# A hybrid trunk on one core: the first MLP's second product as seven block products, with x turned back afterwards

## The chip, the cores and the metric

The kernel runs on one core of one Trainium2 chip. The metric is the device time of one launch in microseconds (us); the kernel before was timed three times, 1201.20, 1201.91 and 1201.94, median 1201.91 us.

## The reference

A decoder trunk of two layers on 512 tokens with 1024 channels, all in fp32. Every mixer and every MLP adds to the residual stream x:

```
x = x + even_mixer(rmsnorm(x))      # an S5 scan and dilated attention, one output projection
x = x + relu(rmsnorm(x) @ w1[0])**2 @ w2[0]
x = x + odd_mixer(rmsnorm(x))       # mLSTM: matrix memory, exponential gates, chunks
x = x + relu(rmsnorm(x) @ w1[1])**2 @ w2[1]
```

w1 is 1024 x 4096 and w2 4096 x 1024 in each layer. The change is in the second line and in the beginning of the third.

## The kernel before, in words

**Data.** x lies in SBUF as eight tiles of 128 channels x 512 tokens (`self.x[k]`, tags x0 to x7). A step `prep(k, gi)` (line 189) makes of a tile the gained hi and lo halves `hg[k]` (ACT line 117, then DVE line 108) and adds its squares to `ss`; the norm's factor itself is applied later, after a product. An fp32 product is the sum of three products in a rounded type: weight hi x activation hi, hi x lo, lo x hi. One such matmul is 128 x 128 weights against 512 columns.

**Weights** come as units of 512 KB (`wr`, 128 x 1024 fp32), in the order of `unit_list`. `w_pump` (line 151) loads up to four units ahead through SP's queue, and splits up to three ahead: ACT makes `wh` (line 120), DVE makes `wl` (line 96). The sets of buffers are taken in turn by the unit's index modulo 3.

**The order** of each engine's instructions is set by a scheduler that simulates the program's timeline when it is built; the code's order is its start. Engines then work through their own queues in that order.

**The first MLP** (`mlp`, line 261) works in two halves of the 4096 hidden channels. 16 units give relu and square of 16 hidden tiles each half, split into `sh` and `sl` at once; 8 pairs of units then give the second product for eight tiles of x, 48 matmuls each, weights stationary. Each result is scaled by `r2` (the squared norm, spread over 128 rows by `norm_finish_sq` and four matmuls) and added to x; in the second half `prep(m, 2)` follows at once, so that the odd layer's input is made tile by tile.

**The second MLP** (`mlp_rows`, line 377) makes all 32 hidden tiles first and keeps them unsplit (`s0` to `s31`). Its second product is turned around: tokens are stationary, weights move, and the result is tokens x channels. It treats hidden tokens and w2 as 2 x 2 blocks and needs seven block products of 96 matmuls in place of eight (`PRODS`, in the order 1, 4, 6, 7, 5, 2, 3). Four of the seven take sums of weight blocks: `t_sums` (line 289) loads four blocks (`tq`), makes four sums on DVE, stores them to DRAM (`T`) and reads them back later as units. `prod_unit` (line 321) splits each activation block into `sp` hi (ACT, line 120) and lo (DVE, line 96) with a ring of five tiles, and updates the raw blocks on DVE for the products to come. `x_rows` (line 303) turns x to token rows with PE transposes (line 307) and `prod_out` (line 345) adds the scaled products to those rows, which are written out as they become whole.

**The odd layer** (`odd`, line 1084) follows a string, `ODD_SEQ` (line 28): `z` is the gates' product, `v0` to `v7` the V units (four units fill four accumulators `acc`, then ACT copies them to V), `N` the norm's finish, `g` the gates, `c` the turn of the gate columns to `col` (lines 1066 and 1068), `q`, `k`, `s`, `n`, `o`, `h` the steps of a head. `q` loads two rows that the gates wrote to DRAM (`na`, `it`); `s` makes the scores' factor `dx` and `qi`. PSUM has four `acc` buffers, two `psa` and two `psb`. `self.skip` (line 83) takes a gap in a pool and clears it on POOL.

Of the kernel before, what the change touches and what calls it, by code (L numbers as in the profile page):

```python
# [9 lines left out]
F32 = mybir.dt.float32  # L10
# [17 lines left out]
ODD_SEQ = ("z0 v0 N0 g0 v1 v2 v3 q0 c0 k0 q1 s0 k1 n0 q2 s1 k2 n1 o0 h0 q3 s2 k3 n2 o1 h1 q4 s3 k4 n3 "  # L28
# [33 lines left out]
class Trunk:  # L62
# [198 lines left out]
    def mlp(self, nxt):  # L261
        with self.tc.tile_pool(name="mp", bufs=1) as mp:
            for half in range(2):
                s = []
                for m in range(16):
                    z = self.proj(self.hg)
                    if half == 0 and m == 1:
                        r2 = self.norm_finish_sq()
                    rr = self.tmp("rr")
                    self.act(rr, z, AF.Relu)  # L270
                    sh = self.t(mp, (P, T), f"sh{m}", F32R)
                    sl = self.t(mp, (P, T), f"sl{m}", F32R)
                    self.act(sh, rr, AF.Square)
                    sf = self.tmp("sf")
                    self.mul(sf, rr, z)
                    self.sub(sl, sf, sh.bitcast(F32))
                    s.append((sh, sl))
                for m in range(KT):
                    o = self.proj(s, first=True, last=False, ks=range(0, 8))
                    self.proj(s, acc=o, first=False, last=True, ks=range(8, 16))  # L280
                    e = self.tmp("ev", bufs=3)
                    self.mul(e, o, r2)
                    self.add(self.x[m], self.x[m], e)
                    if half == 1:
                        self.prep(m, nxt)

    TS_AT = (2, 5, 8, 11, 14, 17, 20, 23)

    def t_sums(self, mp, u):
        q = [self.t(mp, (P, 1024), f"tq{n}", bufs=1) for n in range(4)]  # L290
        for n in range(4):
            self.dma(q[n], self.a["w2s"][n, u])
# [5 lines left out]
        for n, r in ((1, b11), (3, b12), (2, b22), (4, b21)):  # L298
            d = self.t(self.dp, (P, 1024), f"T{n}_{u}", bufs=1)
            self.dma(d, r)  # L300
            self.tq[n, u] = d

    def x_rows(self, i):
# [4 lines left out]
        if n == 0:  # L308
            r = self.tmp(("ss", "r", "sf", "sf")[t], bufs=(1, 1, 2, 2)[t])
        else:  # L310
            r = self.xt(t)
        self.copy_act(r, p)
        self.xr[t, n] = r

# [30 lines left out]
    def prod_out(self, i, accs):  # L345
        def up(t, n, y, c):
            x = self.xr[t, n]
            self.stt(x, y, c[:, t:t + 1], x, ALU.mult, ALU.add)
            if i in self.DONE[t // 2, n]:
                self.dma(self.out[2 * t + n], x)  # L350
# [26 lines left out]
    def mlp_rows(self):  # L377
        self.tq, self.xr, self.pe, self.pv = {}, {}, {}, {}
        with self.tc.tile_pool(name="mp", bufs=1) as mp:
            self.sq = []  # L380
            p1 = None
            for m in range(32):
# [12 lines left out]
                if 2 <= m < 10:  # L395
                    self.x_rows(m - 2)
                if m in self.TS_AT:
                    self.t_sums(mp, self.TS_AT.index(m))
# [3 lines left out]
            self.prod_out(1, p1)  # L402
            for i in self.PRODS[1:]:
# [3 lines left out]
                self.prod_out(i, accs)  # L407

    def rows_units(self):
        a = self.a  # L410
        un = []
        for m in range(32):
            un.append(a["w1"][1, m])
            if m > 16 and m % 2:
                un.append(a["w2s"][0, (m - 17) // 2])
        src = {4: 4, 6: 2, 7: 3, 5: 1, 2: None, 3: None}
        for i in self.PRODS[1:]:
            q = src[i]
            for u in range(8):
                if i == 2:  # L420
                    un.append(a["w2s"][2, u])
                elif i == 3:
                    un.append(a["w2s"][3, u])
                else:
                    un.append(lambda q=q, u=u: self.tq[q, u])
# [515 lines left out]
    def even(self):  # L941
# [4 lines left out]
        with ExitStack() as es:  # L946
# [37 lines left out]
            def s5_done():  # L984
                s5s.close()
                self.ap = es.enter_context(self.tc.tile_pool(name="at", bufs=1))
                self.skip(self.ap, 128)
# [96 lines left out]
    def odd(self):  # L1084
# [4 lines left out]
        self.skip(mp, 96)  # L1089
# [27 lines left out]
        def z_part(_):  # L1117
            z = self.proj(self.hg)
# [111 lines left out]
    def run(self):  # L1230
# [30 lines left out]
        self.hg = [None] * KT  # L1261

# [4 lines left out]
        self.mlp(2)  # L1267
# [5 lines left out]
        self.mlp_rows()  # L1273

    def unit_list(self):
# [8 lines left out]
        mlp = lambda l: [a["w1"][l, h * 16 + m] if ph == 0 else a["w2"][h, m] for h in range(2) for ph in range(2) for m in range(16)]  # L1284
        units += mlp(0)
# [3 lines left out]
        units += self.rows_units()  # L1289
# [115 lines left out]
```

## Time and profile before

| what | value |
|---|---|
| median of 3 runs | 1201.91 us |
| profiled execution | 1202.68 us |
| its span | 1200.9 us |
| TensorE (PE) busy | 1177.3 us, 98% |
| VectorE (DVE) busy | 736.8 us, 61% |
| ScalarE (ACT) busy | 574.4 us, 48% |
| moved by DMA | 170.41 MB, mean 142 GB/s |
| first MLP, first to last matmul | 350.08 us |
| odd layer's mixer up to its output projection | 214.64 us |
| second MLP, first to last matmul | 331.97 us |

The profile is of one execution; the span runs from its first to its last instruction and is 1.8 us shorter than the time of the launch. The page lists busy time by engine, the chain that ended last and the costliest groups; windows give the same counters for a stretch of the span. PE's matmuls overlap, so the record of one (0.39 us) is longer than the step from one to the next. The granted clock is TensorE's, as a share of its full 2.4 GHz.

### The profile page before, as it was taken

What the parts mean: (1) busy time and instruction counts of PE and PEld (TensorE: products, weight loads), DVE (VectorE), ACT (ScalarE), POOL (GpSimd) and SP (SyncE); (2) the same over time, 40 slices, a digit from 0 to 9 for tenths busy, and PEclk for the clock granted to TensorE, in tenths of its full rate; (3) what the DMA queues carried; (4) which work ended last, traced back from release to release, by engine and by line L of the source; (5) the groups of instructions that cost most, each with busy time, mean ns of one, the idle gap of its engine ahead of it and who ended that gap; (6) DMA issues with size and microseconds to landing.
All of it is one profiled execution on the core that took longest, in us unless ns stands there. A gap on an engine that the chain in (4) does not pass through costs nothing.

```text
span 1200.9 us, 15231 instructions
## 1 busy us (share of the span) xinstructions
PE 1177.3 (98%) x5580; PEld 968.8 (81%) x5580; DVE 736.8 (61%) x1307; ACT 574.4 (48%) x1009; POOL 65.4 (5%) x122
## 2 busy tenths in 40 slices
PE   6989999999999999999999999999999999999998
PEld 5868776788888888888888888887888888888887
DVE  8799864554443344435449773874665564477796
ACT  5467777443432133423336554454344344466664
POOL 0522220000000000000010000000000000000000
PEclk9989999999999999999999999999999999999999
DMA  6434522333323333232334333321499995346664
GB/s 233 123 89 124 144 75 62 114 106 94 100 91 102 101 93 104 90 104 89 103 95 152 105 106 106 93 75 45 164 350 365 349 344 176 118 148 195 206 189 157
DMA packets 61196, 170.41 MB, mean 142 GB/s; under 512 B 15481, under 2 KB 16585, under 8 KB 61121
## 3 DMA queue, kind: packets, MB, share of 16 engines
q1 hardware_dynamic: 59904, 168.13, 42.9%
q0 software_dynamic: 1216, 1.31, 0.5%
q8 instruction: 44, 0.72, 0.3%
q14 instruction: 32, 0.25, 0.1%
HBM read 145.78 MB, written 21.53 MB: 139 GB/s over the span
## 4 chain that ended last, share of the span: by engine, by line
PE 93%; DVE 3%; ACT 2%; POOL 1%; issue 1%; DMA 0%; SPq 0%; DVEq 0%; ACTq 0%
PE acc L123 83%; PE psa L123 5%; PE psb L123 3%; DVE wl L96 1%; PE psb L902 1%; POOL rA L547 1%; ACT wh L120 0%; ACT hg L117 0%; DMA wr<-in_w_l 0%; DVE hg L108 0%; PE psb L1212 0%; PE psb L307 0%; DVE x L96 0%; DVE CG L96 0%; PE psb L653 0%
## 5 line engine op out<-in xcount | busy, mean ns | idle before, releaser
L123 PE MATMUL acc<-hg,wh 128*128 128x512 f32 x1616 | 505.8, 393 | 8.9 <-ACT hg L117 8.2
L120 ACT ACTIVATE wh<-wr 128x1024 fp32r<-128x1024 f32 x219 | 231.9, 1060 | 492.0 <-PE acc L123 401.1
L96 DVE TENSOR_TENSOR wl<-wr,wh 128x1024 fp32r<-128x1024 f32 x219 | 268.2, 1226 | 269.1 <-ACT wh L120 268.5
L123 PEld LDWEIGHTS acc<-hg,wh 128*128 128x128 f32 x1616 | 302.4, 189 | 70.8 <-ACT hg L117 8.2
L123 PE MATMUL acc<-hg,wl 128*128 128x512 f32 x808 | 316.8, 392 | 0.6 <-DVE wl L96 0.6
L123 PEld LDWEIGHTS acc<-hg,wl 128*128 128x128 f32 x808 | 152.3, 188 | 32.4 <-DVE wl L96 1.1
L123 PE MATMUL acc<-wh,sp 128*128 128x512 f32 x384 | 111.4, 389 | 0.0
L123 PE MATMUL acc<-sh,wh 128*128 128x512 f32 x256 | 99.6, 389 | 0.0
L123 PE MATMUL acc<-sl,wh 128*128 128x512 f32 x256 | 99.6, 389 | 0.0
L123 PE MATMUL acc<-sh,wl 128*128 128x512 f32 x256 | 99.6, 389 | 0.0
L123 PEld LDWEIGHTS acc<-wh,sp 128*128 128x128 f32 x384 | 72.1, 188 | 15.0
L123 PE MATMUL acc<-wh,hg 128*128 128x512 f32 x192 | 63.2, 404 | 5.5 <-ACT wh L120 5.5
L123 PE MATMUL acc<-wl,sp 128*128 128x512 f32 x192 | 67.9, 390 | 0.4 <-DVE wl L96 0.4
L123 PEld LDWEIGHTS acc<-sl,wh 128*128 128x128 f32 x256 | 48.0, 188 | 10.1
L123 PEld LDWEIGHTS acc<-sh,wl 128*128 128x128 f32 x256 | 48.0, 188 | 9.9
L123 PEld LDWEIGHTS acc<-sh,wh 128*128 128x128 f32 x256 | 48.0, 188 | 9.9
L96 DVE TENSOR_TENSOR tq<-tq,tq 128x1024 f32<-128x1024 f32 x32 | 39.1, 1223 | 20.1 <-DMA tq<-in_w2s 19.7
L123 PEld LDWEIGHTS acc<-wh,hg 128*128 128x128 f32 x192 | 37.0, 194 | 13.4 <-ACT wh L120 5.9
L120 ACT ACTIVATE sp<-s 128x256 fp32r<-128x256 f32 x112 | 44.6, 408 | 1.9 <-PE acc L123 1.3
L96 DVE TENSOR_TENSOR ev<-acc,r 128x512 f32<-128x512 f32 x16 | 11.1, 692 | 53.3 <-PE acc L123 53.3
L96 DVE TENSOR_TENSOR sp<-s,sp 128x256 fp32r<-128x256 f32 x112 | 43.5, 418 | 0.3 <-ACT sp L120 0.3
L123 PEld LDWEIGHTS acc<-wl,sp 128*128 128x128 f32 x192 | 36.0, 188 | 8.2 <-DVE wl L96 0.8
(318 smaller groups left out, 1491.5 us busy)
## 6 DMA issues: line engine op xcount, KB each, us to landing
wr<-in_w SPq DMA_DIRECT2D x96, 512.0 KB, 3.5
wr<-in_w_l SPq DMA_DIRECT2D x67, 512.0 KB, 3.5
tq<-in_w2s SPq DMA_DIRECT2D x32, 512.0 KB, 6.3
T<-tq SPq DMA_DIRECT2D x32, 512.0 KB, 5.0
wr<-T SPq DMA_DIRECT2D x32, 512.0 KB, 3.4
wr<-in_w2s SPq DMA_DIRECT2D x24, 512.0 KB, 4.0
x<-in_xT SPq DMA_DIRECT2D x16, 256.0 KB, 4.7
na<-scr SPq DMA_DIRECT2D x8, 256.0 KB, 4.3
```

The costliest lines, as they stand in the source:

```text
L96: return self.nc.vector.tensor_tensor(out=o, in0=x, in1=y, op=op)
L120: return self.nc.scalar.activation(o, x, AF.Copy)
L123: return self.nc.tensor.matmul(o, l, r, start=start, stop=stop)
L547: gt = lambda o, x, y, op: self.nc.gpsimd.tensor_tensor(out=o, in0=x, in1=y, op=op)
L902: self.nc.tensor.transpose(t[:, k * P:(k + 1) * P], p[:, k * P:(k + 1) * P], self.ident)
```

## The change

`mlp` now is what `mlp_rows` was, called for both layers. In layer 0, after products 2 and 3, `x_back` turns the finished rows back to tiles of x: 16 PE transposes each time, four copies by ACT, and `prep(k, 2)` for each tile. `t_sums`, the unit list and the weights' layout get a layer index; `z` has its accumulator in `psa`; the odd layer's string begins with two V units; the gap of 128 bytes in the attention's pool goes and the one in the odd layer's pool shrinks from 96 to 32 bytes. In the first MLP, PE's 768 matmuls of the second product become 672, with 32 transposes to rows and 32 back; the units go from 64 to 88, with 32 loads of `tq` and 32 stores of `T` beside them.

```diff
--- before.py
+++ after.py
@@ -25,7 +25,7 @@
 RSQ = float(0x5F3759DF)
 
 
-ODD_SEQ = ("z0 v0 N0 g0 v1 v2 v3 q0 c0 k0 q1 s0 k1 n0 q2 s1 k2 n1 o0 h0 q3 s2 k3 n2 o1 h1 q4 s3 k4 n3 "
+ODD_SEQ = ("v0 v1 z0 N0 g0 v2 v3 q0 k0 q1 c0 s0 k1 n0 q2 s1 k2 n1 o0 h0 q3 s2 k3 n2 o1 h1 q4 s3 k4 n3 "
            "v4 v5 v6 v7 o2 h2 q5 s4 k5 n4 o3 h3 q6 s5 k6 n5 o4 h4 q7 s6 k7 n6 o5 h5 o6 s7 h6 n7 o7 h7")
 EVEN_SEQ = ("u0 C0 a0 K0 E0 b0 u1 n0 T0 a2 C1 u2 E1 v0 v1 K1 C2 u3 E2 v2 B0 B1 v3 O0 K2 T1 b2 n2 a1 r0 C3 B2 r2 E3 a3 b1 B3 O1 K3 b3 "
             "h0 n3 h1 G0 n1 h2 h3 T2 h4 X h5 h6 h7 T3 G1 r1 h8 h9 h10 h11 h12 r3 O2 h13 h14 h15 h16 h17 h18 O3 h19 h20 h21 h22 h23 h24 h25 h26 h27 h28 "
@@ -258,49 +258,23 @@
         return self.spread(rc2)
 
 
-    def mlp(self, nxt):
-        with self.tc.tile_pool(name="mp", bufs=1) as mp:
-            for half in range(2):
-                s = []
-                for m in range(16):
-                    z = self.proj(self.hg)
-                    if half == 0 and m == 1:
-                        r2 = self.norm_finish_sq()
-                    rr = self.tmp("rr")
-                    self.act(rr, z, AF.Relu)
-                    sh = self.t(mp, (P, T), f"sh{m}", F32R)
-                    sl = self.t(mp, (P, T), f"sl{m}", F32R)
-                    self.act(sh, rr, AF.Square)
-                    sf = self.tmp("sf")
-                    self.mul(sf, rr, z)
-                    self.sub(sl, sf, sh.bitcast(F32))
-                    s.append((sh, sl))
-                for m in range(KT):
-                    o = self.proj(s, first=True, last=False, ks=range(0, 8))
-                    self.proj(s, acc=o, first=False, last=True, ks=range(8, 16))
-                    e = self.tmp("ev", bufs=3)
-                    self.mul(e, o, r2)
-                    self.add(self.x[m], self.x[m], e)
-                    if half == 1:
-                        self.prep(m, nxt)
-
     TS_AT = (2, 5, 8, 11, 14, 17, 20, 23)
 
-    def t_sums(self, mp, u):
+    def t_sums(self, mp, l, u):
         q = [self.t(mp, (P, 1024), f"tq{n}", bufs=1) for n in range(4)]
         for n in range(4):
-            self.dma(q[n], self.a["w2s"][n, u])
+            self.dma(q[n], self.a["w2s"][l, n, u])
         b11, b12, b21, b22 = q
         self.sub(b11, b12, b11)
         self.sub(b12, b22, b12)
         self.sub(b22, b22, b11)
         self.sub(b21, b22, b21)
         for n, r in ((1, b11), (3, b12), (2, b22), (4, b21)):
-            d = self.t(self.dp, (P, 1024), f"T{n}_{u}", bufs=1)
+            d = self.t(self.dp, (P, 1024), f"T{l}_{n}_{u}", bufs=1)
             self.dma(d, r)
-            self.tq[n, u] = d
-
-    def x_rows(self, i):
+            self.tq[l, n, u] = d
+
+    def x_rows(self, l, i):
         n, t = i // 4, i % 4
         p = self.psb()
         for k in range(4):
@@ -308,9 +282,29 @@
         if n == 0:
             r = self.tmp(("ss", "r", "sf", "sf")[t], bufs=(1, 1, 2, 2)[t])
         else:
-            r = self.xt(t)
+            r = self.xt(4 * l + t)
         self.copy_act(r, p)
         self.xr[t, n] = r
+
+    def x_cols(self, k):
+        n = k // 4
+        p = self.psb() if k % 2 == 0 else self.psa()
+        for t in range(4):
+            self.nc.tensor.transpose(p[:, t * P:(t + 1) * P], self.xr[t, n][:, (k % 4) * P:(k % 4 + 1) * P], self.ident)
+        return p
+
+    def x_back(self, n):
+        p = {}
+        for k in range(4 * n, 4 * n + 4):
+            p[k] = self.x_cols(k)
+            if n == 0:
+                self.x[k] = self.xt(4 + k)
+                self.copy_act(self.x[k], p[k])
+        for k in range(4 * n, 4 * n + 4):
+            if n == 1:
+                self.x[k] = self.xt(k - 4)
+                self.copy_act(self.x[k], p[k])
+            self.prep(k, 2)
 
...
@@ -342,11 +336,11 @@
                 self.mm(accs[m], sh[:, ms], l[:, s], False, False)
                 self.mm(accs[m], sl[:, ms], h[:, s], False, k == 15)
 
-    def prod_out(self, i, accs):
+    def prod_out(self, i, accs, last):
         def up(t, n, y, c):
             x = self.xr[t, n]
             self.stt(x, y, c[:, t:t + 1], x, ALU.mult, ALU.add)
-            if i in self.DONE[t // 2, n]:
+            if last and i in self.DONE[t // 2, n]:
                 self.dma(self.out[2 * t + n], x)
 
         for m in range(2):
@@ -374,8 +368,8 @@
     PRODS = (1, 4, 6, 7, 5, 2, 3)
     DONE = {(0, 0): (2,), (0, 1): (3,), (1, 0): (7,), (1, 1): (5,)}
 
-    def mlp_rows(self):
-        self.tq, self.xr, self.pe, self.pv = {}, {}, {}, {}
+    def mlp(self, l):
+        self.xr, self.pe, self.pv = {}, {}, {}
         with self.tc.tile_pool(name="mp", bufs=1) as mp:
             self.sq = []
             p1 = None
@@ -393,36 +387,38 @@
                 self.act(s, rr, AF.Square)
                 self.sq.append(s)
                 if 2 <= m < 10:
-                    self.x_rows(m - 2)
+                    self.x_rows(l, m - 2)
                 if m in self.TS_AT:
-                    self.t_sums(mp, self.TS_AT.index(m))
+                    self.t_sums(mp, l, self.TS_AT.index(m))
                 if m > 16 and m % 2:
                     p1 = p1 or [self.psa(), self.psa()]
                     self.prod_unit(mp, 1, (m - 17) // 2, p1)
-            self.prod_out(1, p1)
+            self.prod_out(1, p1, l)
             for i in self.PRODS[1:]:
                 accs = [self.acc(), self.acc()]
                 for u in range(8):
                     self.prod_unit(mp, i, u, accs)
-                self.prod_out(i, accs)
-
-    def rows_units(self):
+                self.prod_out(i, accs, l)
+                if l == 0 and i in (2, 3):
+                    self.x_back(i - 2)
+
+    def mlp_units(self, l):
         a = self.a
         un = []
         for m in range(32):
-            un.append(a["w1"][1, m])
+            un.append(a["w1"][l, m])
             if m > 16 and m % 2:
-                un.append(a["w2s"][0, (m - 17) // 2])
+                un.append(a["w2s"][l, 0, (m - 17) // 2])
         src = {4: 4, 6: 2, 7: 3, 5: 1, 2: None, 3: None}
         for i in self.PRODS[1:]:
             q = src[i]
             for u in range(8):
                 if i == 2:
-                    un.append(a["w2s"][2, u])
+                    un.append(a["w2s"][l, 2, u])
                 elif i == 3:
-                    un.append(a["w2s"][3, u])
+                    un.append(a["w2s"][l, 3, u])
                 else:
-                    un.append(lambda q=q, u=u: self.tq[q, u])
+                    un.append(lambda q=q, u=u: self.tq[l, q, u])
         return un
...
@@ -984,7 +980,6 @@
             def s5_done():
                 s5s.close()
                 self.ap = es.enter_context(self.tc.tile_pool(name="at", bufs=1))
-                self.skip(self.ap, 128)
 
             def glu():
                 self.s5_glu(zp)
@@ -1086,7 +1081,7 @@
         es = ExitStack()
         mp = es.enter_context(self.tc.tile_pool(name="ml", bufs=1))
         ot = es.enter_context(self.tc.tile_pool(name="mo", bufs=1))
-        self.skip(mp, 96)
+        self.skip(mp, 32)
         self.gb = self.t(mp, (8, 2), "gb")
         self.rst = self.t(mp, (8, T), "rst")
         self.cvw = self.t(mp, (P, 16, 4), "cvw")
@@ -1115,7 +1110,7 @@
                     self.act(V[:, b, :, 0:P], accs[b].rearrange("p (h e) -> p h e", e=P), AF.Copy, scale=self.rc[:, b:b + 1])
 
         def z_part(_):
-            z = self.proj(self.hg)
+            z = self.proj(self.hg, acc=self.psa())
             self.gz = self.tmp("ev", bufs=3)
             self.copy_act(self.gz[0:40], z[0:40])
 
...
@@ -1281,12 +1277,11 @@
                 i = {"u": n, "v": 12 + n, "a": 4 + 2 * (n % 2) + 4 * (n // 2), "b": 5 + 2 * (n % 2) + 4 * (n // 2)}[step[0]]
                 units.append(a["w_l0"][i])
         units += [a["w_l0"][i] for i in range(16, 26)]
-        mlp = lambda l: [a["w1"][l, h * 16 + m] if ph == 0 else a["w2"][h, m] for h in range(2) for ph in range(2) for m in range(16)]
-        units += mlp(0)
+        units += self.mlp_units(0)
         base = {"z": 0, "v": 1, "q": 9, "k": 17, "o": 25}
         units += [a["w_l1"][base[step[0]] + int(step[1:])] for step in ODD_SEQ.split() if step[0] in base]
         units += [a["w_l1"][33 + m] for m in range(8)]
-        units += self.rows_units()
+        units += self.mlp_units(1)
         return units
 
     def x_load(self, ks):
@@ -1327,8 +1322,7 @@
     ws.append(std(np.concatenate([wo[0:512][perm], wo[512:]], 0)))
     a["w_l0"] = cc(np.concatenate(ws, 0))
     a["w1"] = cc(np.stack([std(i["mlp_w1"][l]) for l in range(2)]))
-    a["w2"] = cc(i["mlp_w2"][0].reshape(2, 2, 8, P, 8, P).transpose(0, 4, 1, 3, 2, 5).reshape(2, 16, P, 1024))
-    a["w2s"] = cc(i["mlp_w2"][1].reshape(2, 8, 2, P, 2, T).transpose(0, 4, 1, 3, 2, 5).reshape(4, 8, P, 1024))
+    a["w2s"] = cc(i["mlp_w2"].reshape(2, 2, 8, 2, P, 2, T).transpose(0, 1, 5, 2, 4, 3, 6).reshape(2, 4, 8, P, 1024))
 
     w = i["od_w_in"][0]
     gw = np.zeros((D, P), f)
```

In the first MLP as built, three of the four first subtractions on `tq` stand in DVE's order ahead of `wl` of the third unit; in the second MLP two do.

**PE, from the end of the first MLP into the odd layer.** Before (`acc_4837` is the last product, `acc_4930` the gates' z):

```order
L123 MATMUL acc_4837<-sh_876_4348,wh_4771 128x512
L123 MATMUL acc_4837<-sl_877_4349,wh_4771 128x512
L123 MATMUL acc_4837<-sh_876_4348,wl_4772 128x512
L123 MATMUL acc_4930<-hg_4418,wh_4801 128x512 x2
L123 MATMUL acc_4930<-hg_4418,wl_4802 128x512
```

After (`acc_5224` and `acc_5225` are product 3, `acc_5492` and `acc_5493` two of V's accumulators, `psb` and `psa` take the turned tiles):

```order
L123 MATMUL acc_5225<-wl_5325,sp_5409 128x512
L123 MATMUL acc_5224<-wh_5324,sp_5409 128x512
L123 MATMUL acc_5225<-wh_5324,sp_5409 128x512
L123 MATMUL acc_5492<-wl_5349,hg_5204 128x512
L123 MATMUL acc_5492<-wh_5348,hg_5204 128x512
L123 MATMUL acc_5493<-wl_5349,hg_5204 128x512
```

and, at the last of the 22 matmuls of v0 and v1 that stand here:

```order
L123 MATMUL acc_5493<-wl_5373,hg_5204 128x512
L123 MATMUL acc_5493<-wh_5372,hg_5204 128x512
L293 MATMUL psb_5420<-cst_83,x_623_2904 128x128
L293 MATMUL psa_5425<-cst_83,x_623_2904 128x128
L293 MATMUL psb_5430<-cst_83,x_623_2904 128x128
L293 MATMUL psb_5420<-cst_83,x_631_2946 128x128
```

22 matmuls of v0 and v1 now stand between the last product and the 16 transposes; 24 more of them follow the transposes, then z.

**ACT, in product 3 of the first MLP.** Before, at the end of the first MLP (one `prep` after every second split):

```order
L120 ACTIVATE wh_4771<-wr_4730 128x1024
L120 ACTIVATE wh_4801<-wr_4769 128x1024
L117 ACTIVATE hg_4418<-x_499_2231,gain_71 128x512
L117 ACTIVATE ev_4834<-x_499_2231 128x512
L120 ACTIVATE wh_4840<-wr_4799 128x1024
```

After (`sp` are the hi halves that product 3 needs, `x_1085` to `x_1091` the copies of the first turn):

```order
L120 ACTIVATE sp_5328<-s_807_3789 128x256
L120 ACTIVATE x_1085_5181<-psb_5176 128x512
L120 ACTIVATE x_1087_5188<-psa_5183 128x512
L120 ACTIVATE x_1089_5195<-psb_5190 128x512
L117 ACTIVATE hg_5204<-x_1085_5181,gain_71 128x512
L117 ACTIVATE ss_5207<-x_1085_5181 128x512
L120 ACTIVATE x_1091_5202<-psa_5197 128x512
L117 ACTIVATE hg_5204<-x_1087_5188,gain_71 128x512
L117 ACTIVATE ev_5211<-x_1087_5188 128x512
L117 ACTIVATE hg_5204<-x_1089_5195,gain_71 128x512
L117 ACTIVATE ev_5216<-x_1089_5195 128x512
L120 ACTIVATE sp_5337<-s_813_3824 128x256
```

Four copies, three hi halves and three squares stand between two `sp` halves that follow one another; the row ahead of the piece is a weight split, `wh_5252`.

**DVE, in the odd layer at the first scores.** Before (`col` are the gate columns, `qi` needs the row `it` from DRAM):

```order
L1068 COPY col_5219<-psb_5214 128x288
L108 SCALAR_TENSOR_TENSOR sf_5205<-zb_5202,cvw_4917,sf_5205 128x512
L108 SCALAR_TENSOR_TENSOR dx_5320<-na_5198,col_5219,cmask_4920 128x128 x4
L108 SCALAR_TENSOR_TENSOR dx_5476<-na_5295,col_5219,cmask_4920 128x128 x4
L108 SCALAR_TENSOR_TENSOR sf_5205<-zb_5202,cvw_4917,sf_5205 128x512
L96 TENSOR_TENSOR zb_5252<-acc_5221,r_5023 128x512
L96 TENSOR_TENSOR wl_5225<-wr_5168,wh_5224 128x1024
L108 SCALAR_TENSOR_TENSOR q_5212<-rr_5210,sf_5205 128x512
L108 SCALAR_TENSOR_TENSOR sf_5255<-zb_5252,cvw_4917,sf_5255 128x512
L96 TENSOR_TENSOR qi_5329<-q_5212,it_5199 128x384
```

After:

```order
L108 SCALAR_TENSOR_TENSOR q_5774<-rr_5772,sf_5767 128x512
L1063 COPY col_5871<-psb_5866 128x288
L108 SCALAR_TENSOR_TENSOR sf_5810<-zb_5807,cvw_5479,sf_5810 128x512
L96 TENSOR_TENSOR qi_5891<-q_5774,it_5761 128x384
L108 SCALAR_TENSOR_TENSOR dx_5882<-na_5760,col_5871,cmask_5482 128x128 x4
L108 SCALAR_TENSOR_TENSOR dx_6038<-na_5850,col_5871,cmask_5482 128x128 x4
L108 SCALAR_TENSOR_TENSOR sf_5857<-zb_5854,cvw_5479,sf_5857 128x512
```

`qi` moved from the tenth place of the piece to the second behind `col`, ahead of both groups of `dx`.

## Rows read from the trace of the kernel before

**Rows 1.** The page: busy time of the engines, and the chain that ended last by engine.

```profile
PE 1177.3 (98%) x5580; PEld 968.8 (81%) x5580; DVE 736.8 (61%) x1307; ACT 574.4 (48%) x1009; POOL 65.4 (5%) x122
...
PE 93%; DVE 3%; ACT 2%; POOL 1%; issue 1%; DMA 0%; SPq 0%; DVEq 0%; ACTq 0%
```

**Rows 2.** Windows: first MLP, odd mixer, second MLP. us, engines' busy, PEclk, DMA share, GB/s.

```profile
255.83:605.91 350.08, 350.08 (x1553) 290.07 (x1552) 150.50 (x177) 115.10 (x146) 0.52 (x1) 1.00 0.31 98
605.91:820.55 214.64, 214.64 (x1095) 182.10 (x1094) 152.05 (x288) 110.79 (x228) 14.58 (x34) 1.00 0.33 102
864.93:1196.90 331.97, 331.57 (x1481) 274.02 (x1479) 216.33 (x321) 170.90 (x274) 0.00 (x0) 1.00 0.69 238
```

**Rows 3.** Waits of PE in the second MLP: us in total, times, longest.

```profile
PE acc L123 <- DVE wl L96: 0.4, 1, 0.4
```

**Rows 4.** Window: the last 16 us of the first MLP.

```profile
589.82:605.91 16.09, 16.09 (x72) 13.33 (x71) 6.24 (x7) 4.23 (x5) 0.00 (x0) 1.00 0.32 99
```

**Rows 5.** PE's timeline around four transposes in the second MLP: start, us, instruction.

```profile
882.22 0.60 PE L307 MATMUL psb<-cst,x 128*128 128x128 f32 x4
882.57 0.70 PE L123 MATMUL acc<-hg,wh 128*128 128x512 f32 x2
883.11 0.39 PE L123 MATMUL acc<-hg,wl 128*128 128x512 f32 x1
```

**Rows 6.** Line 307 whole: count, min/median/max ns of a record, first and last start.

```profile
L307 PEld LDWEIGHTS psb<-cst,x x32: 138/140/142, 882.0 to 923.8; 128*128 128x128 f32 x32
L307 PE MATMUL psb<-cst,x x32: 270/272/273, 882.2 to 923.9; 128*128 128x128 f32 x32
```

**Rows 7.** ACT's groups in the second MLP: busy us, mean ns | idle before.

```profile
L120 ACT ACTIVATE wh<-wr 128x1024 fp32r<-128x1024 f32 x86 | 91.3, 1061 | 155.4 <-PE acc L123 134.3 <-DMA wr<-in_w2s 8.6 <-issue 8.5
...
L120 ACT ACTIVATE x<-psb 128x512 f32<-128x512 f32 x4 | 2.4, 592 | 0.0
```

**Rows 8.** The groups of `prep` over the whole span.

```profile
L108 DVE SCALAR_TENSOR_TENSOR hg<-x,gain,hg 128x512 fp32r<-128x512 f32 x32 | 23.5, 745 | 0.0
L117 ACT ACTIVATE hg<-x,gain 128x512 fp32r<-128x512 f32 x32 | 22.6, 712 | 4.6 <-DVE x L96 4.6
...
L96 DVE TENSOR_TENSOR ss<-ss,ev 128x512 f32<-128x512 f32 x28 | 19.2, 685 | 0.0
...
L117 ACT ACTIVATE ev<-x 128x512 f32<-128x512 f32 x28 | 17.2, 616 | 0.7 <-DVE ss L96 0.7
```

**Rows 9.** Window: product 3 of the second MLP.

```profile
1175.20:1196.90 21.70, 21.70 (x96) 17.64 (x94) 14.78 (x25) 10.04 (x18) 0.00 (x0) 1.00 0.43 145
```

**Rows 10.** DVE's timeline: the two updates of x behind product 3.

```profile
1196.52 1.41 DVE L108 SCALAR_TENSOR_TENSOR x<-acc,rc,x 128x512 f32<-128x512 f32 x2 [4.72 <-PE acc L123]
```

**Rows 11.** DVE's timeline: the second weight sum of the second MLP, and the split behind it.

```profile
873.29 1.23 DVE L96 TENSOR_TENSOR tq<-tq,tq 128x1024 f32<-128x1024 f32 x1 [2.01 <-DMA tq<-in_w2s]
874.44 1.22 DVE L96 TENSOR_TENSOR wl<-wr,wh 128x1024 fp32r<-128x1024 f32 x1
```

**Rows 12.** Timelines of ACT, PE, SP and DVE: the gates of the odd layer.

```profile
624.96 0.60 ACT L120 ACTIVATE r<-psb 128x512 f32<-128x512 f32 x1 [0.51 <-PE psb L123]
...
638.80 1.29 ACT L117 ACTIVATE pk<-ev 8x512 f32<-8x512 f32 x2
...
642.25 0.41 PE L1066 MATMUL psb<-cst,pk 72*128 72x72 f32 x4
...
644.49 0.80 SPq L126 DMA_DIRECT2D it<-scr  x2
...
650.42 0.55 DVE L96 TENSOR_TENSOR qi<-q,it 128x384 f32<-128x384 f32 x1
```

**Rows 13.** The page, DMA issues: count, KB each, us from issue to landing.

```profile
na<-scr SPq DMA_DIRECT2D x8, 256.0 KB, 4.3
```

**Rows 14.** Windows in the second MLP: its first 135 us, and the slowest piece of 25.

```profile
864.93:1000.00 135.07, 135.07 (x617) 111.97 (x616) 80.42 (x91) 60.30 (x91) 0.00 (x0) 1.00 0.95 346
950.00:975.00 25.00, 25.00 (x112) 20.70 (x111) 15.16 (x17) 10.40 (x15) 0.00 (x0) 1.00 0.90 328
```

More of the change, by code (lines that the diff above doesn't have):

```diff
@@ L1261, in run @@
         self.hg = [None] * KT
+        self.tq = {}
         self.even()
@@ L1266, in run @@
         self.wp2 = self.ctx.enter_context(self.tc.tile_pool(name="wp2", bufs=1))
-        self.mlp(2)
+        self.mlp(0)
         if self.stop == "l0":
@@ L1272, in run @@
             return self.finish()
-        self.mlp_rows()
+        self.mlp(1)
     def unit_list(self):
```

## The prediction

> **What bounds the kernel now.** I read the page first. TensorE (PE) is busy in 98% of the span and makes 93% of the chain that ended last; VectorE (DVE) stands at 61% and ScalarE (ACT) at 48% [rows 1]. So what counts is the time of PE's own instructions and the few places where PE waits. The windows by stage come next: the first MLP has 350.08 us with PE busy for all of it, the odd layer's mixer 214.64 us likewise, the second MLP 331.97 us with 331.57 busy; the granted clock is 1.00 of the full 2.4 GHz in all three [rows 2]. The table of waits puts one wait of 0.4 us into the second MLP, for a split weight of DVE's [rows 3]; for the first MLP it is empty. The two MLPs have the same shapes, so the second one, which computes its second product as seven block products already, is a measured copy of what the first one becomes. The forecast rests on that, and the work is in what the copy lacks and what stands around it.
>
> The profiled execution took 1202.68 us, 0.77 more than the median of 1201.91. I add my difference, taken from stages of that execution, to the median.
>
> **The change part by part.** *First MLP in the second one's form.* 350.08 becomes 331.97, which is -18.11 us; the copy's wait of 0.4 is inside. The count of instructions agrees. 96 matmuls of 512 columns go (768 become 672). Before the stage ends, 71 weight loads and so 71 matmuls take 16.09 us [rows 4], 0.2266 each, so 96 are 21.8 us. The form adds 32 transposes of x to token rows. Four of them with two matmuls behind take from 882.22 to 883.11, 0.89 us [rows 5]; less 2 x 0.2266 that leaves 0.44, or 0.11 each, so 32 are 3.5 us. -21.8 + 3.5 = -18.3, against -18.11 by stages.
>
> *Turning x back.* The second MLP needs no such step, since it writes its rows out. The changed kernel adds 32 transposes, 16 after product 2 and 16 after product 3: +3.5 us at 0.11. Here is the first choice. The row has four in a run and the change has sixteen. Below stands a quarter of a matmul by columns, 0.2266/4 = 0.057 (-1.7 us for all); above stands the weight load of each, 0.140 [rows 6], if sixteen in a run are held to it (+1.0 us). I take 0.11, the only pace seen. The record of one transpose, 272 ns [rows 6], is no pace, since records overlap; it is a rival below.
>
> *What the first turn holds up.* After product 2, ACT gets four copies out of PSUM (0.592 each), four hi halves (0.712) and four squares (0.616), and DVE four lo halves (0.745) and three sums (0.685) [rows 7, 8]. In ACT's order, the copies and three each of the hi halves and squares stand between two neighbouring `sp` halves: 4 x 0.592 + 3 x 0.712 + 3 x 0.616 = 6.35 us. PE has 28 matmuls before it needs the later `sp`, 28 x 0.2266 = 6.35 us. That is even, but a split weight of 1.06 us [rows 7] stands ahead on ACT, and I judge that ACT begins about 0.9 late. By sums the stretch fits: the same stretch of the second MLP (product 3) has 21.70 us with DVE busy for 14.78 and ACT for 10.04 [rows 9]; with 4 x 0.745 + 3 x 0.685 = 5.0 more DVE has 19.8, with 4 x (0.592 + 0.712 + 0.616) = 7.7 more ACT has 17.7. So it is one short wait and no shift of the bound: +0.8 us, between 0 (the ring of five `sp` tiles covers it) and 2.0 (one more split weight, 1.06, comes late too).
>
> *What the second turn holds up: nothing.* Product 3's last matmul is followed by 22 matmuls of the V units v0 and v1 that need only hg[0..3], which the first turn made: 5.0 us. In that time DVE must do the two updates of x, 1.41 us [rows 10], with up to two weight splits of 1.22 [rows 11] ahead: 3.9 us. Behind the 16 transposes come 24 more such matmuls and 12 of z, 8.2 us, before hg[4] is read; four copies, one hi and one lo take 3.8 us. If that cover were gone, the whole chain of 3.9 + 3.8 us would be bare. PSUM: V holds the four `acc` buffers, so z moves to `psa`, and q0's accumulator waits for V's copies on ACT, with nine matmuls of z and the spread between (2.8 us). SP's queue takes the T stores and loads as in the second MLP; POOL's constants for the odd layer are asked for where they were. The dropped gap is a memset on POOL, busy 5% of the span [rows 1]. These edits together: 0, with no gain possible, as PE waits for none of them now.
>
> *Start of the first MLP.* Three subtractions of weight blocks stand on DVE ahead of `wl` of the third unit; in the second MLP two do, the second ending 9.6 us after the stage's start and `wl` 10.7 us after [rows 11]. One more makes 11.9. PE asks for it after 59 matmuls, 13.4 us. Cost 0, bound 0.5.
>
> *The odd layer's gates.* z runs after v0 and v1. The copy of the spread norm ended at 625.56, the exponentials of the gates at 640.09, 14.5 us later, and PE turned the gate columns at 642.25, 16.7 us after the copy [rows 12]. Now 79 matmuls stand between, 17.9 us: 3.4 to spare. Then it is DVE's turn: `qi`, the product that needs the `it` row brought back from DRAM, now stands two behind `col`, ahead of `dx`. Before, the load was issued at 644.49, 18.9 us after the copy, and `qi` ran at 650.42, unwaited [rows 12]. A row of that kind lands 4.3 us after its issue [rows 13], so 23.2 us after the copy, and DVE is there after 20 to 22 (`col` at 18 to 19, 1.2 for it and one convolution, up to one split of 1.22). It may idle 1 to 3 us with `dx` behind it; PE has about one us of matmuls before it needs the next thing from DVE. Cost 0 to 2.2; I take 0, since `qi` had 1.6 us to spare before and the same steps of the chain lead to it, and keep 2.2 as rival A.
>
> **Sum**: -18.11 + 3.5 + 0.8 = -13.8; 1201.91 - 13.8 = **1188.1 us**.
>
> **The rivals.** *Likeliest (0.71):* every cover holds; its own range is 1186.6 to 1189.6.
>
> *A, the wait moves into DVE's queue in the odd layer (0.16).* DVE sits at `qi` for the `it` row, and `dx` and the scores behind it make PE wait: up to 2.2 us, 1190.3. For it speaks the new order; against it, that DVE is busy 71% of that stage (152.05 of 214.64) [rows 2].
>
> *B, transposes cost their record (0.03).* If the 32 new ones cost 0.272 in place of 0.11, +5.2, 1193.3. Against it: four of them and two matmuls fit into 0.89 us [rows 5], and the stage with 32 is still 18 us shorter. The Trainium skill ("TensorE: Matmul & The Clock Gate", Part 4: PE-mode transpose) gives about 275 ns for one in a kernel and says that transposes don't count as busy for the clock. The trace agrees on the record (272 ns), not on the pace, and the stage with 32 transposes has a granted clock of 1.00.
>
> *C, the other side: transfers become the bound of the first MLP (0.04).* Its first 135 us now move what the second's move: 346 GB/s at a DMA share of 0.95, 46.7 MB, where the stage had 98 GB/s at 0.31 [rows 2, 14]. PE there waits once for 0.4 us. From first to last matmul, the stage can stretch to 148.9 us before it eats the 13.8 gained, that is 314 GB/s; at 300 it takes 155.7, +20.6, and the time is 1208.7, slower. For it: the queue is busy 0.90 to 0.95 of it. Against it: the same bytes in the same order reach 328 GB/s even in the slow piece [rows 14]. Of the 0.04 I give 0.03 to slower and 0.01 to no change. The Trainium skill ("SBUF — State Buffer", its table of bandwidths) gives about 358 GB/s between HBM and a core; the row's 346 is 0.97 of it, so by it nothing more would fit, and nothing more is asked.
>
> *D, cheaper still (0.06).* The first turn holds up nothing (-0.8), the copy's wait of 0.4 goes, and the 32 transposes run nearer to their columns, at 0.08 (-1.0): 1185.9.
>
> **How the numbers follow.** The point is the likeliest case. Low end 1185.6, just under D. High end: 1188.1 + 1.2 (first turn at 2.0) + 2.2 (A) + 0.5 (tq) + 1.0 (transposes at 0.140) = 1193.0. That leaves out C and most of B. A measurement here tells 0.2%, 2.4 us. Faster: likeliest, A, B and D, 0.96; same 0.01; slower 0.03.
>
> **What would show it.** First MLP 334 to 337 us, with 64 transposes in it and around its end; PE waits in product 3 of 1 us or less, for `sp` or a split; none between product 3 and z; odd layer within 1 us of 214.6; granted clock 1.00; DMA share near 0.95 in the first 135 us of the first MLP, `wr` still landing in 3 to 6 us. I am wrong if the first MLP shows waits for `wr` or `tq` of several us (C), if PE idles behind `dx` or `qi` (A), or if sixteen transposes in a run take over 2.3 us (B).

## The result, and the profile after

The changed kernel takes 1186.45 us (median of 4, 1185.93 to 1188.18), the kernel before on the same chips 1201.93: ratio 0.987, 95% interval 0.986 to 0.989, or -15.5 us. The forecast was -13.8, 1188.1 us, with a range from 1185.6 to 1193.0. The profiled execution took 1185.93 with a span of 1184.1.

The page of the changed kernel, busy time and the chain, to be set beside [rows 1]:

```profile
span 1184.1 us, 15701 instructions
...
PE 1161.5 (98%) x5540; PEld 956.2 (81%) x5540; DVE 813.4 (69%) x1466; ACT 643.1 (54%) x1162; POOL 64.1 (5%) x121
...
PE 92%; DVE 3%; ACT 1%; POOL 1%; issue 1%; DMA 1%; SPq 0%; DVEq 0%; ACTq 0%
```

PE is still the bound; DVE and ACT took up 77 and 69 us more beside it and have room left. The windows by stage (first MLP, odd mixer, odd output projection, second MLP; columns as in [rows 2]):

```profile
253.29:587.26 333.97, 333.57 (x1500) 276.23 (x1499) 223.70 (x330) 179.91 (x289) 0.52 (x1) 1.00 0.69 238
587.26:804.08 216.82, 216.27 (x1110) 183.56 (x1108) 155.36 (x295) 114.73 (x238) 13.20 (x34) 1.00 0.33 106
804.08:848.11 44.03, 43.59 (x194) 35.13 (x192) 23.44 (x34) 17.90 (x33) 1.01 (x1) 1.00 0.29 96
848.11:1180.07 331.96, 331.56 (x1481) 274.02 (x1479) 216.35 (x321) 170.96 (x274) 0.00 (x0) 1.00 0.69 238
```

The first MLP became 350.08 - 333.97 = 16.11 us shorter, the odd mixer, which now holds the second turn, 2.18 us longer; the second MLP is as it was. The odd layer's output projection took 44.38 us before:

```profile
820.55:864.93 44.38, 43.95 (x194) 35.15 (x192) 23.45 (x34) 17.92 (x33) 1.01 (x1) 1.00 0.29 95
```

Now it takes 44.03, or -0.35. The first MLP starts at 253.29 instead of 255.83: -2.54 us in a layer that the change hardly touches. The sum is -2.54 - 16.11 + 2.18 - 0.35 = -16.8, the difference of the spans (1200.9 to 1184.1); 1.3 us of it belong to the two executions, since the medians differ by 15.5.

PE's waits in the changed kernel: the first MLP, the odd mixer, the second MLP.

```profile
PE acc L123 <- DVE wl L96: 0.4, 1, 0.4
...
PE acc L123 <- ACT V L117: 0.6, 1, 0.6
...
PE acc L123 <- DVE wl L96: 0.4, 1, 0.4
```

Neither turn of x is among them. The first MLP now has the same 0.4 us as the second [rows 3]; new is one wait of 0.6 in the odd layer, at the second set of V.

PE's timeline at the second turn, after product 3, from the last of the V matmuls that cover it:

```profile
592.02 0.39 PE L123 MATMUL acc<-wh,hg 128*128 128x512 f32 x1
592.24 0.27 PE L293 MATMUL psb<-cst,x 128*128 128x128 f32 x1
...
593.55 0.60 PE L293 MATMUL psa<-cst,x 128*128 128x128 f32 x4
593.91 0.47 PE L123 MATMUL acc<-wh,hg 128*128 128x512 f32 x1
```

Sixteen transposes take 593.91 - 592.24 = 1.67 us, 0.104 each, with no idle time before or behind. Two points of the forecast stay open: the 2.5 us in the even layer, and whether the reasons given for "nothing" were the reasons.

### The profile page after: what moved, and what is told of

The parts are those of the page before. It is cut to its first block, busy times and chain, and to the rows that moved or that the text cites. A ratio compares the mean times of both kernels' runs of the same rounds, so it can differ in the third digit from the quotient of the medians.

```text
span 1184.1 us, 15701 instructions
## 1 busy us (share of the span) xinstructions
PE 1161.5 (98%) x5540; PEld 956.2 (81%) x5540; DVE 813.4 (69%) x1466; ACT 643.1 (54%) x1162; POOL 64.1 (5%) x121
## 4 chain that ended last, share of the span: by engine, by line
PE 92%; DVE 3%; ACT 1%; POOL 1%; issue 1%; DMA 1%; SPq 0%; DVEq 0%; ACTq 0%
PE acc L123 79%; PE psa L123 8%; PE psb L123 3%; DVE wl L96 1%; PE psb L898 1%; POOL rA L543 1%; PE psb L281 1%; ACT wh L120 0%; ACT hg L117 0%; DVE hg L108 0%; DMA hg<-in_amask 0%; DMA wr<-in_w_l 0%; DVE x L108 0%; PE psb L1207 0%; DVE x L96 0%
## 5 line engine op out<-in xcount | busy, mean ns | idle before, releaser
L123 PE MATMUL acc<-wh,sp 128*128 128x512 f32 x768 | 223.0, 389 | 0.0
L123 PEld LDWEIGHTS acc<-wh,sp 128*128 128x128 f32 x768 | 144.2, 188 | 30.0
L123 PE MATMUL acc<-wl,sp 128*128 128x512 f32 x384 | 135.9, 390 | 0.8 <-DVE wl L96 0.8
L120 ACT ACTIVATE sp<-s 128x256 fp32r<-128x256 f32 x224 | 89.8, 409 | 6.8 <-PE acc L123 5.7
L96 DVE TENSOR_TENSOR tq<-tq,tq 128x1024 f32<-128x1024 f32 x64 | 78.2, 1222 | 21.0 <-DMA tq<-in_w2s 20.0
L96 DVE TENSOR_TENSOR sp<-s,sp 128x256 fp32r<-128x256 f32 x224 | 86.8, 417 | 1.4 <-ACT sp L120 1.4
L123 PE MATMUL psa<-wh,sp 128*128 128x512 f32 x128 | 42.0, 389 | 0.0
L117 ACT ACTIVATE rr<-acc 128x512 f32<-128x512 f32 x72 | 41.6, 578 | 0.0
L117 ACT ACTIVATE s<-rr 128x512 f32<-128x512 f32 x64 | 40.4, 631 | 1.0
L123 PE MATMUL acc<-wl,hg 128*128 128x512 f32 x96 | 38.5, 401 | 0.3 <-DVE wl L96 0.3
```

The source lines that it names most:

```text
L96: return self.nc.vector.tensor_tensor(out=o, in0=x, in1=y, op=op)
L117: return self.nc.scalar.activation(o, x, f, bias=bias, scale=scale, **kw)
L120: return self.nc.scalar.activation(o, x, AF.Copy)
L123: return self.nc.tensor.matmul(o, l, r, start=start, stop=stop)
```

## The experiments

Two theories for the even layer stand against each other: that the gaps in the pools, which the forecast put at nothing, change PE's pace by moving its operands; or that two executions merely differ. Six runs are on this, four on the forecast's covers and on rival C.

**One gap put back**, in the changed kernel:

```diff
                 self.ap = es.enter_context(self.tc.tile_pool(name="at", bufs=1))
+                self.skip(self.ap, 128)
```

> The change with the gap of 128 bytes in the attention's pool put back; it moves four pairs of tiles (yh4 to yl7) and nothing else. Theory 'address' (the gap sets where these moving operands start, and that sets PE's pace in the even layer's output projection): a matmul there takes 0.232 us as in the kernel before, not 0.227, and the 40 us of that projection grow by 0.8 to 1.1 us. Rival 'chance' (two executions simply differ there): 0.227 per matmul, no growth. The whole time is 1187.4 by the first, 1186.5 by the second, which timing alone would not tell apart.

1186.52 us in one run. A measure of pace that doesn't hang on when the stage began: DVE makes eight additions of the even output projection's results to x, one for each 24 matmuls, and from the first one's start to the last one's PE works through 150 of them. Each line has count, shortest, median and longest record in ns, and the first and the last start. Before, after, and with the gap put back:

```profile
L96 DVE TENSOR_TENSOR x<-x,acc x8: 680/689/689, 220.6 to 256.0; 128x512 f32<-128x512 f32 x8
```

```profile
L96 DVE TENSOR_TENSOR x<-x,acc x8: 679/687/689, 218.8 to 253.5; 128x512 f32<-128x512 f32 x8
```

```profile
L96 DVE TENSOR_TENSOR x<-x,acc x8: 680/687/690, 218.6 to 254.0; 128x512 f32<-128x512 f32 x8
```

35.4, 34.7 and again 35.4 us. The slow pace comes back with the gap: "address". The 0.7 us are those of 150 matmuls, while 0.8 to 1.1 was expected of the whole projection. From the layer's first matmul on a `y` tile to the first MLP's first it is 0.9: 72.13 us before (183.70 to 255.83), 71.28 in the change (182.01 to 253.29), 72.16 with the gap back (181.63 to 253.79). The eight other runs without a gap here lie between 71.23 and 71.30, so this is no chance difference of two executions.

**A gap of 64 in its place:**

```diff
                 self.ap = es.enter_context(self.tc.tile_pool(name="at", bufs=1))
+                self.skip(self.ap, 64)
```

> The change with a gap of 64 bytes in the attention's pool. Theory 'address': the even output projection is slower than with no gap, 0.229 to 0.232 us per matmul, since these tiles then stand as the odd layer's output tiles stood in the kernel before (0.229 there). Rival 'chance': 0.227.

1187.55 us in one run, and the eight additions:

```profile
L96 DVE TENSOR_TENSOR x<-x,acc x8: 682/689/689, 219.5 to 254.9; 128x512 f32<-128x512 f32 x8
```

35.4 us: 64 bytes off cost as much here as 128.

**The norm's output moved:** `hg` starts 128 bytes later, and 128 bytes behind it make 256 for all that follows.

```diff
         self.hp = self.ctx.enter_context(self.tc.tile_pool(name="hp", bufs=1))
+        self.skip(self.hp, 128)
...
             self.hgs = self.t(self.hp, (P, 16, T), "hg", F32R, 1)
+            if gi == 0:
+                self.nc.gpsimd.memset(self.t(self.hp, (P, 32), "skip2", F32, 1), 0.0)
```

> The change with the norm's output hg moved by 128 bytes, and everything behind it by 256; the same work otherwise. hg is the moving operand of about 2400 matmuls. Theory 'address': each takes 0.0045 to 0.009 us more, so +11 to +22 us, 1197 to 1208; the first product of both MLPs goes from 0.227 to 0.232 per matmul or more. Rival 'chance': 1186.5, 0.227.

1199.88 us (10 runs, 1199.58 to 1200.94; ratio to the kernel before 0.9987, 0.9978 to 0.9996): 13.4 us slower than the change, most of its gain gone. Two memsets are all that was added, and PE's waits add up to 18.5 us against 18.6 in the change. The 32 reads of the first product by ACT in the second MLP, first and last start, in the change and here:

```profile
L117 ACT ACTIVATE rr<-acc x32: 574/575/583, 856.8 to 1046.9; 128x512 f32<-128x512 f32 x32
```

```profile
L117 ACT ACTIVATE rr<-acc x32: 576/582/583, 866.0 to 1060.5; 128x512 f32<-128x512 f32 x32
```

190.1 against 194.5 us: 4.4 more over 31 x 24 = 744 matmuls, 0.0059 each, 2.6% of 0.2267. "Address" is shown, for the largest group of matmuls in the program.

A rival is that `hg`, once moved, collides with what other engines read and write. Two windows of the same product in which DVE, ACT and POOL do nothing, in the change and here:

```profile
1029.52:1032.28 2.76, 2.76 (x14) 2.29 (x13) 0.00 (x0) 0.00 (x0) 0.00 (x0) 1.00 0.60 190
```

```profile
1042.69:1045.61 2.92, 2.92 (x14) 2.37 (x13) 0.00 (x0) 0.00 (x0) 0.00 (x0) 1.00 0.51 180
```

Eleven steps of PE take 2.49 us in the first (1029.60 to 1032.09) and 2.57 in the second (1042.84 to 1045.41), 0.227 and 0.234 each. The slow pace stands with DVE, ACT and POOL idle, so they are not its cause; nor does it follow the transfers, for from 919.39 to 922.84, at a DMA share of 0.96, a step takes 0.233 as well. The even projection, whose tiles here lie 256 further from the weights, kept its fast 34.7 us:

```profile
L96 DVE TENSOR_TENSOR x<-x,acc x8: 678/688/689, 219.6 to 254.3; 128x512 f32<-128x512 f32 x8
```

**All moved together**, behind the first pool:

```diff
         nc.gpsimd.memset(self.pwh, -0.5)
+        self.skip(self.cp, 64)
```

> The change with 64 bytes put ahead of every pool but the first, so that weights, activations and all else move by 64 together. Theory 'absolute' (a moving operand is slower from some starts, whatever the weights' start): nearly all of the 128x512 matmuls take about 0.0055 us more, as in the run with hg moved, +15 to +22 us. Theory 'relative' (what counts is the distance between the moving operand and the weights): nothing changes, 1186.5.

1188.01 us (4 runs, 1185.95 to 1188.22; ratio 0.9886, 0.9871 to 0.9901). The reads of the first product and the eight additions:

```profile
L117 ACT ACTIVATE rr<-acc x32: 575/575/582, 859.0 to 1049.1; 128x512 f32<-128x512 f32 x32
```

```profile
L96 DVE TENSOR_TENSOR x<-x,acc x8: 682/687/689, 220.5 to 255.2; 128x512 f32<-128x512 f32 x8
```

190.1 and 34.7 us, the fast values; the median is 1.6 us above the change's, inside the spread of both, where "absolute" asked for 15 to 22. The four pairs of tiles of the even projection start here where they did with the gap of 64 alone, at 35.4 us; what differs is that everything they are read with moved too. So it isn't the start as such but the distance to something else: "relative". That the something is the weights follows by elimination, since PE reads nothing else in these matmuls and the other engines and the transfers are not the cause; no run moved the weights alone. With the 256 of the run before, which cost nothing, and the 64 and 128 that did, the distance seems to count modulo 256.

**The gaps alone**, in the kernel before:

```diff
-                self.skip(self.ap, 128)
...
-        self.skip(mp, 96)
+        self.skip(mp, 32)
```

> The kernel before with the two pool gaps of the change and nothing else of it. Theory 'address': the even output projection loses 0.8 to 1.1 us and the odd one 0.3 to 0.5, so -1.1 to -1.6 us, about 1200.5; that is 0.1% and near the limit of the timing, the two stretches of the trace must show it (0.227 per matmul in both). Rival 'chance', and my own forecast, which put the gaps at nothing: 0, with 0.232 and 0.229 per matmul.

1200.21 us (11 runs) against 1201.53 (21 runs): -1.3, ratio 0.999, 0.9981 to 0.9999. The eight additions of the even projection, then of the odd one:

```profile
L96 DVE TENSOR_TENSOR x<-x,acc x8: 679/686/689, 219.7 to 254.4; 128x512 f32<-128x512 f32 x8
...
L96 DVE TENSOR_TENSOR x<-x,acc x8: 680/688/690, 833.8 to 863.2; 128x512 f32<-128x512 f32 x8
```

34.7 and 29.4 us, against 35.4 and 29.6 in the kernel before. The gaps make 0.1% by themselves, just clear of the noise.

**The odd gap put back**, in the changed kernel:

```diff
-        self.skip(mp, 32)
+        self.skip(mp, 96)
```

> The change with the odd layer's gap back at 96 bytes, which moves its tiles (mh, ml, q, k and others) by 64 and nothing else. Theory 'relative' (a moving tile that does not start at the same distance as the weights modulo 256 makes its matmuls slower): the odd output projection's eight additions spread over 29.6 us as in the kernel before, not 29.4, and the whole is 0.2 to 0.5 us longer; the even one keeps its 34.7. Rival 'chance': 29.4.

1186.45 us in one run; even projection, odd projection:

```profile
L96 DVE TENSOR_TENSOR x<-x,acc x8: 680/687/689, 218.7 to 253.4; 128x512 f32<-128x512 f32 x8
...
L96 DVE TENSOR_TENSOR x<-x,acc x8: 679/686/689, 819.1 to 848.8; 128x512 f32<-128x512 f32 x8
```

34.7 and 29.7, where the change has 29.4: 0.3 us of the odd projection, as "relative" has it; the whole is within the noise. 64 bytes cost less here than in the even layer, for twice as many moved tiles. What distance costs how much is not settled.

**The cover of the second turn taken away.** Products 2 and 3 change places, so that V's first units read the half of x that is turned last; `prep` and `sumsq` begin with tile 4 there.

```diff
-    PRODS = (1, 4, 6, 7, 5, 2, 3)
+    PRODS = (1, 4, 6, 7, 5, 3, 2)
...
-            elif i == 2:
+            elif i == 5:
                 self.sub(c, c, d)
+            elif i == 3:
+                self.add(c, c, d)
```

> The change with products 2 and 3 in the other order in both MLPs, so that the half of x that the V units v0 and v1 read is turned back last (16 updates of s move from product 2 to 5, 16 additions come behind product 3 to undo them; the sums are the same up to rounding). In PE's order the second 16 transposes then stand right behind the last product and the V units right behind them. Theory 'cover' (22 V matmuls on the half turned first hide the updates, 24 and z's 12 hide the copies and halves): the chain is bare, 1.4 to 3.9 us for DVE's two updates and 1.3 to 3.8 us of copies and halves on ACT and DVE before and between the first V matmuls, so +3 to +7.7 us, 1189.5 to 1194. Rival 'hidden anyway' (the chain is short enough, or other work fills it): under +1, 1187.5.

1190.69 us (4 runs, 1190.21 to 1191.88; ratio 0.9913, 0.9896 to 0.9929): +4.2 to the change. PE's waits from product 2's end into the odd layer:

```profile
PE acc L123 <- ACT hg L117: 1.8, 1, 1.8
PE psb L293 <- DVE ss L108: 1.2, 1, 1.2
PE psa L123 <- DVE k L108: 1.1, 1, 1.1
PE psa L123 <- DVE dx L108: 0.2, 1, 0.2
```

1.2 for the update ahead of the transposes, 1.8 for the copy and hi half behind them: 3.0 us of the chain come out bare, at the low end of what was priced. "Cover" is shown by these two waits. The other 1.3, at the first scores, come later in DVE's order, and the edit also gave DVE 16 additions more, so they can't be put down to the cover alone.

**The old beginning of the odd layer's string**, in the changed kernel:

```diff
-ODD_SEQ = ("v0 v1 z0 N0 g0 v2 v3 q0 k0 q1 c0 s0 k1 n0
+ODD_SEQ = ("z0 v0 N0 g0 v1 v2 v3 q0 c0 k0 q1 s0 k1 n0
```

> The change with the odd layer's string begun as before (z0 v0 N0 g0 v1 ... q0 c0 k0); z keeps its accumulator in psa. In the order as built the scheduler itself puts V matmuls ahead of the second turn, but 12 of them instead of 22. Theory 'cover': 12 are 2.7 us, DVE needs 1.4 to 3.9 before the first transposes, so PE waits 0 to 1.2 us there and nothing else changes: 1186.5 to 1187.7. Rival 'the string is what hides the turn': z first leaves the chain bare, +3 us or more, 1189.5.

1187.23 us (4 runs, 1186.62 to 1188.09; ratio 0.9884, 0.9869 to 0.9898): not to be told from the change. PE waits 0.2 us, for a weight split, in the whole stretch from 560 to 640. As expected the scheduler puts V matmuls ahead of the turn here too, 12 where the change has 24, so the string isn't what hides it.

**Rival C: more transfers.** Each `tq` of the first MLP is loaded twice in the first run, four times (the edit here) in the second.

```diff
         for n in range(4):
+            for _ in range(3 if l == 0 else 0):
+                self.dma(q[n], self.a["w2s"][l, n, u])
             self.dma(q[n], self.a["w2s"][l, n, u])
```

> The change with each of the 32 loads of weight blocks (tq) of the first MLP made twice: 16.8 MB more in its first 135 us, 63.5 MB where 46.7 MB moved at a DMA share of 0.95. Theory 'transfers stand next behind PE' (346 to 370 GB/s is all the queue gives): those bytes need 172 to 184 us, and PE waits 35 to 50 us in the first MLP, for wh and wl whose wr comes late: 1220 to 1237. Rival 'there is room': the loads overlap, below +5 us.

1186.7 us in one run: nothing lost, and the theory fell. Windows of the change and of this kernel, in the first 137 us of the first MLP and the 70 behind them:

```profile
253.00:390.00 137.00, 137.00 (x625) 113.65 (x625) 82.37 (x93) 60.94 (x92) 0.00 (x0) 1.00 0.94 346
...
390.00:460.00 70.00, 70.00 (x310) 57.95 (x309) 32.61 (x53) 33.77 (x52) 0.52 (x1) 1.00 0.37 119
```

```profile
253.00:390.00 137.00, 137.00 (x626) 113.65 (x625) 69.04 (x81) 60.95 (x92) 0.00 (x0) 1.00 0.94 353
390.00:460.00 70.00, 70.00 (x311) 57.96 (x310) 42.96 (x59) 33.92 (x53) 0.52 (x1) 1.00 0.88 332
```

The queue is at 0.94 in both and PE busy throughout. The extra bytes ran on into the next 70 us, where the share rose from 0.37 to 0.88. What is due early (w1's units) still came in time; what came late (the sums) is read from product 4 on.

> The change with each tq load of the first MLP made four times: 50.3 MB more than the change has. With the loads twice nothing was lost: the sums went on to 460 us (382 in the change) beside the later stretch, where the queue had room, and PE reads the last sum of product 4 only at about 455. Theory 'due date' (the sums have until product 4, and only then do transfers bind): 33.6 MB more at 330 to 370 GB/s are 90 to 100 us beyond that date, so PE waits 75 to 105 us in product 4, none of it before 430 us: 1261 to 1292. Theory 'transfers stand next behind PE in the first 135 us' (my rival C) would have PE wait there, for w1's units; theory 'the queue gives way anyway': under +20 us.

1280.78 us in one run, +94.3. PE waits in two stretches, 253 to 430 (none) and 430 to 700:

```profile
PE acc L123 <- ACT wh L120: 82.0, 4, 25.1
```

what ACT waited for with those splits, from 430 to 600 (`T` are the sums),

```profile
ACT wh L120 <- DMA wr<-T: 77.0, 6, 23.6
```

and the window of the second stretch's beginning:

```profile
430.00:560.00 130.00, 52.02 (x193) 39.64 (x191) 46.58 (x67) 22.80 (x38) 0.52 (x1) 0.68 0.91 345
```

The four waits end at 482.7, 511.1, 541.5 and 564.1, at the last four units of product 4, as "due date" says, and behind them stand the sums. The date itself was set too early: in the change product 4 runs from 453.73 to 475.49, so its last sum is due about 473, not 455. To the 82 us comes PE's clock: PE waited up to 25.1 us at a time, and the granted clock of this stretch is 0.68 of full, a mean of both levels (1.2 and 2.4 GHz), where it was 1.00 before the waits.

## Why the prediction was right, and where not

The change is -15.5 us where -13.8 was forecast, inside the range but 0.15 us under the likeliest case's own (1186.6 to 1189.6). That is not case D: the first turn did hold up nothing, but the 0.4 us wait stayed and a transpose took 0.104, not 0.08. The rest came from the pool gaps, which the forecast had at 0; without their 1.3 us the time would be about 1187.8.

- *The second MLP as a copy*: right. From first to last matmul the first MLP now takes 333.74 us (253.29 to 587.03), the second 331.60 (848.11 to 1179.71). Sixteen transposes (1.66) and two V matmuls that the scheduler drew in (0.45) make the difference.
- *0.11 per transpose*: right, 0.104 in a run of sixteen (1.67 us, where rival B asked for over 2.3). The Trainium skill ("TensorE: Matmul & The Clock Gate", Part 4: PE-mode transpose) gives about 275 ns for one in a kernel; the trace agrees on the record, 270 to 273 here, yet one follows the other after 0.104. Rival B falls.
- *The first turn, +0.8*: too much; it cost no wait. The step that failed is the sum of records. Here each instruction of ACT starts before the record of the one ahead ends (a copy of 0.57 us at 570.60, the next at 571.08), so the ten between two `sp` halves took 575.91 - 570.60 = 5.31 us, not 6.35:

```profile
570.60 0.57 ACT L120 ACTIVATE x<-psb 128x512 f32<-128x512 f32 x1
571.08 0.58 ACT L120 ACTIVATE x<-psa 128x512 f32<-128x512 f32 x1
...
575.91 0.42 ACT L120 ACTIVATE sp<-s 128x256 fp32r<-128x256 f32 x1
```

- *The second turn, nothing*: right, and for the reason given: with the cover taken away PE waits 3.0 us on the chain, and the kernel takes 4.2 more.
- *The first MLP's start*: right; `wl` ended 12.05 us after it, 11.9 was forecast.
- *The gates and `qi`* (rival A): DVE did sit there for 2.26 us, inside the forecast 1 to 3, and PE had no wait from it. The cover held.

```profile
642.76 0.56 DVE L96 TENSOR_TENSOR qi<-q,it 128x384 f32<-128x384 f32 x1 [2.26 <-DMA it<-scr]
```

- *The pool gaps, "0, with no gain possible, as PE waits for none of them"*: wrong. PE's pace is no wait and stands in no table of waits. The step that failed is to price an edit by the waits it can end; what the runs show instead is that the gaps shift moving tiles and with them PE's pace in the products that read them. They give 1.2 us by the trace (0.85 in the even layer, 0.35 in the odd projection) and 1.3 by time.
- *Rival C*: its chance was small, its price was wrong. 314 GB/s was no break-even: bytes moved in a stretch are not the bytes due in it. Twice the loads cost nothing; four times cost 94.3 us, with all waits for the sums in product 4 and none in the first 135 us.
- Not foreseen: the wait of 0.6 us at V, behind ACT's copies. It returns with 0.55 us in every run of the changed kernel except the one with products 2 and 3 exchanged; the old string has it too, so the string's beginning is not its cause, which stays open.

So the forecast missed 0.8 (first turn) and 1.2 to 1.3 (gaps), and the V wait took back 0.6: -13.8 becomes -15.2 to -15.3. Of the even layer's 2.54 us in the profiles, 0.85 are the gap; 1.06 lie before PE's first matmul (8.22 and 7.16 us; other executions had 7.1 to 8.4), which is no work of the change. The remaining 0.63 lie between that matmul and the first on `y` (175.48 and 174.84 us); the other runs have 174.4 to 176.4 there, so nothing is explained by it.

## What to carry to other kernels

Where a stage exists twice, a measured copy gives the price, and counting checks it (-18.11 and -18.3 here); price what the copy lacks, and look for the work that hides it, then try the kernel without that cover. An edit that only moves tiles is not free because nobody waits for them: compare the step from one matmul to the next. Sum starts, not records, when instructions of one engine stand in a row. A transfer queue near 1.0 says little until it is known when its bytes are due.

## What the runs showed of the hardware

PE's pace depends on where the moving operand lies in SBUF relative to what it is read with, by elimination the weights. With `hg` 128 bytes off, a 128x512 matmul takes 0.0059 us more and the program 13.4, also where DVE, ACT and POOL are idle; with all moved alike by 64 bytes the pace is the fast one. The Trainium skill ("SBUF — State Buffer", Who interferes with whom) has the moving operand and the weight load read through independent ports and says that PE never waits on anyone; the runs differ from it by this 2.6%, and the measurement decides.
